# Score buffers of an attention kernel in one PSUM tile, with a table for the order of all engines

## The chip, the core and the metric

The kernel runs on one core of a Trainium2 chip. A core has engines that each work through their own queue of instructions in order: TensorE (PE; its weight loads, PEld, run beside its matmuls), VectorE (DVE), ScalarE (ACT), GpSimd (POOL) and SyncE (SP), whose queue only starts transfers here. An instruction that has to wait for another engine holds up everything behind it in its own queue. The metric is the device time of one execution in microseconds (us); lower is better.

## What is computed

Plain attention for 8 batches of 8 heads, 512 positions and 64 dimensions, float32 in and out:

```python
scale = 1.0 / np.sqrt(q.shape[-1])
scores = np.einsum('bhqd,bhkd->bhqk', q, k) * scale
scores = scores - scores.max(axis=-1, keepdims=True)
attn = np.exp(scores)
attn = attn / attn.sum(axis=-1, keepdims=True)
return np.einsum('bhqk,bhkd->bhqd', attn, v).astype(np.float32)
```

## The kernel before

The 64 heads are taken two at a time: 32 pairs, numbered 0 to 31, with heads a and b. For each pair SP loads q, k and v (256 KB each). POOL casts them to 16 bits. PE transposes q and k (line 558), DVE copies the transposes out of PSUM (L571), and PE computes scores.

A block of scores is 128 keys by 512 queries of one head. Two blocks are a *group*, two PSUM banks of 512 columns each, and all further work goes by groups. They are numbered 0 to 128; the last two are the two halves of one group of scores. Two matmuls write a group (L598). Then it is read in one of two ways:

- ScalarE takes the exponential of all 1024 columns in one instruction and writes 16-bit weights `pt` (L602). The first groups have their own lines (L801).
- For 16 of the groups VectorE does it instead. The list `ON_DVE` names them. One instruction, called *raise* here (`raise_`, L625), reads the scores from PSUM and writes `pd`, and five *passes* (L642 to L665), from and to SBUF, turn `pd` into two factors `pe` and `pd` of the exponential.

PE multiplies the weights with v (L704; v carries a column of ones, so the sums of the weights come along). DVE takes the reciprocal of the sums (L671) and multiplies (L676), and SP stores the result. For the very last head the products land in a tile `o_last` (L720, L734).

PSUM has eight banks. Three buffers of two banks hold scores; two single banks are shared by transposes and products. So at most three groups of scores exist at once, and the matmuls of a group wait until the group three before it has been read. Each of the three buffers is a tile of its own from a pool:

```python
ps_st = ctx.enter_context(tc.tile_pool(name="ps_st", bufs=3, space=bass.MemoryType.PSUM))
...
st = ps_st.tile([P, 2, S], FP32, tag="st", name=f"st_{m}")
```

Waits are not written in the kernel. A layer below it looks at which instruction writes and reads which tile, and puts in a wait on a semaphore wherever two engines touch the same tile in a way that it takes for a dependence. An instruction that comes later in the program waits for the earlier one, never the other way round.

The order of each queue is the order in which the program issues its instructions. The class `Plan` makes it: it steps through an imagined time with a cost for each kind of step and writes down a list of steps, such as "scores of group 40" or "raise of group 39". A step "scores" issues the two matmuls and at once the ScalarE exponential. A step "raise" issues the VectorE read.

Of the kernel before, what the change touches and what calls it, by code (L numbers as in the profile page):

```python
# [17 lines left out]
class Plan:  # L18

    SLOT, EXP, EXP_DONE, EXP_FIXED = 216, 853, 181, 64  # L20
    INTO, OUT_OF = 96, 96
    TRANSPOSE, V_UNIT = 222, 128
    TO_ACT, TO_DVE, TO_PE = 220, 210, 60

    COPY, NORM, RAISE = (601, 690), (50, 133), (1132, 1215)
    RECIPROCAL = 115
    SCALE, PRODUCT, EXTRA = 333, 600, 29
    COPY_1 = (400, 190)
    NORM_COLUMN, PASS_DONE = 67, 115
    PASSES = (SCALE, SCALE, PRODUCT, SCALE, PRODUCT)  # L30
    BITS = 2
    NEEDS = (None, None, 0, 2, 3)
    FIRST_EXP = 5000
    STEP = 5
    CALM, KEEN = 9000, 4
    FIRST_UNIT = 4
    KNOWN, OVER = (13, 15, 18, 20, 22, 24, 27, 42, 50, 61, 69, 97), 6
    ON_DVE = (5, 10, 16, 25, 28, 39, 44, 54, 63, 66, 74, 81, 91, 96, 103, 116)

    LATE_NORM, LATE_COPY, HURRY, SOON, BACKLOG = 700, 1500, 800, 160, 600  # L40
    LATE_MUL, WAIT = 400, 200
    SLACK, AHEAD = 0, 2

    CAST, CAST_PORT, CAST_DONE, TO_POOL = 557, 475, 130, 150
    SCALE_PORT, PRODUCT_PORT, GAP, REACH = 271, 537, 20, 5
    FIRST_LAND, LOAD, STORE, LATENCY, ISSUE = 5200, 752, 376, 2300, 470
    QUEUED, URGENT = 3500, 16
    PAIRED, STORE_ISSUE = 18, 520
    RAW, QK16, NV, NU = 7, 5, 12, 112
    PAIR, DUEK, DUEV, DUEL, PRE = 3300, 3550, 6000, 5000, 0  # L50

    def __init__(self, groups, pairs, first):
        self.groups, self.pairs = groups, pairs
        self.pe, self.act, self.dve = 7000, self.FIRST_EXP, 6300
        self.pool, self.port, self.dma = 4600, 4600, self.FIRST_LAND
        self.m, self.tiled = first, True
        self.read = []
        self.exps = {}
        for m in range(first):
            self.act += self.EXP + self.EXP_FIXED  # L60
            self.exps[m] = self.act + self.EXP_DONE
            self.read.append(self.exps[m])
        self.tq = {0: 5800}
        self.transposed = {0: 5800}
        self.next_t = 1
        self.part_t = 0
        self.banks = [5100, 5800]
        self.todo = [(g, h) for g in range(pairs) for h in range(2)]
        self.last = self.todo.pop()
        self.last_part = 0  # L70
        self.head = None
        self.units = self.FIRST_UNIT
        self.member = {b: m for m, grp in enumerate(groups) for b in grp}
        self.ready = []
        self.passes = []
        self.passed = {}
        self.raised = set()
        self.steps = []
        self.busy_dve = 0
        self.order, self.paired = [], 0  # L80

        late = {grp[0][0] for m, grp in enumerate(groups) if m in self.ON_DVE}
        due = []
        for g in range(pairs):
            scores = 5000 + self.PAIR * g
            if g:
                due += [(scores - self.DUEK, g, "k"), (scores - self.DUEK + 10, g, "q")]
            due.append((scores + self.DUEV + (self.DUEL if g in late else 0), g, "v"))
        self.due = sorted(due)
        self.uncast = list(self.due)  # L90
        self.casts = []
        self.landed, self.cast_done = {}, {}
        self.first_loads = [(g, n) for _, g, n in self.due if g < self.RAW]
        self.first_loads += [(self.RAW, "k"), (self.RAW, "q")]
        for x in self.first_loads:
            self.dma += self.LOAD
            self.landed[x] = self.dma
        self.loads, self.stores, self.stored = [], [], []
        self.sp = 1650 + 470 * len(self.first_loads)

    def note(self, t, *what):
        self.steps.append((t, len(self.steps)) + what)

    def trigger(self, t):

        ops = self.ops
        if not ops or ops[-1][1] <= t - 300:  # L110
            return 1, None
        n = len(ops) - 1
        while (
            n > 0
            and len(ops) - n < self.REACH
            and not ops[n][2]
            and ops[n][0] - ops[n - 1][1] <= self.GAP
        ):
            n -= 1
        if n > 0 and ops[n][0] - ops[n - 1][1] <= self.GAP:  # L120
            n -= 1
        return len(ops) - n, ops[n][1]

    def emit(self, t, back, after):
        _, g, n = self.uncast.pop(0)
        shared = (g, n) == (1, "q")
        self.note(t, "cast", g, n, back if t > self.CALM else 0)
        if not shared:
            self.casts.append((g, n, t if after is None else after + self.TO_POOL))
        if g + self.RAW < self.pairs:  # L130
            self.loads.append((g + self.RAW, n))

    def fits(self, t, soon=0):
        if not self.uncast:
            return False
        _, g, n = self.uncast[0]
        if n != "v" and g >= self.QK16 and self.transposed.get(g - self.QK16, 1e9) > t:
            return False
        return self.landed.get((g, n), 1e9) <= t + soon

    def step_pool(self, t):
        if self.uncast and self.uncast[0][1:] != (1, "q") and not self.casts and self.pool <= t:
            quiet = not self.passes and self.port <= t and not any(x[1] == "raise" for x in self.ready)
            if self.fits(t) and (quiet or self.uncast[0][0] - self.PRE < t):
                self.emit(t, 1, None)
        if self.casts and self.pool <= t and self.port <= t:
            g, n, after = self.casts[0]
            if after <= t and self.landed.get((g, n), 1e9) <= t:
                self.casts.pop(0)
                begin = max(self.pool, self.port, after, self.landed[(g, n)])  # L150
                self.pool = begin + self.CAST
                self.port = begin + self.CAST_PORT
                self.cast_done[(g, n)] = begin + self.CAST + self.CAST_DONE

    def step_sp(self, t):
        if self.sp > t or (self.loads and self.dma > t + self.QUEUED):
            return
        urgent = len(self.stores) > self.URGENT
        if self.loads and not urgent:
            g, n = self.loads[0]  # L160
            if self.cast_done.get((g - self.RAW, n), 1e9) <= t:
                self.loads.pop(0)
                self.note(t, "load", g, n)
                self.dma = max(self.dma, t + self.LATENCY - self.LOAD) + self.LOAD
                self.landed[(g, n)] = self.dma
                self.sp = t + self.ISSUE
                return
        if self.stores and self.stores[0] <= t:
            both = self.both()
            if both and (len(self.stores) < 2 or self.stores[1] > t):  # L170
                return
            heads = 2 if both else 1
            self.note(t, "store", heads)
            self.dma = max(self.dma, t + self.LATENCY - heads * self.STORE) + heads * self.STORE
            for _ in range(heads):
                self.stores.pop(0)
                self.stored.append(self.dma)
            self.paired += heads - 1
            self.sp = t + self.STORE_ISSUE

    def both(self):

        n = len(self.stored)
        g, h, u = self.order[n]
        return (
            self.paired < self.PAIRED
            and g < self.pairs - 2
            and h == 0
            and n + 1 < len(self.order)
            and self.order[n + 1][0] == g  # L190
            and u % self.NU + 8 <= self.NU
        )

    def room(self, t, u):
        heads = (u - self.NU - self.FIRST_UNIT + 3) // 4
        return heads <= 0 or len(self.stored) >= heads and self.stored[heads - 1] <= t

    def free(self, n=0):
        m = self.m + n
        if m >= len(self.groups):  # L200
            return 1e9
        g = self.groups[m][0][0]
        return max(0 if m < 3 else self.read[m - 3], self.tq.get(g, 1e9))

    def for_dve(self, m):
        return m in self.ON_DVE
# [692 lines left out]
```

## Time and profile before

| | |
|---|---|
| time, median of 3 runs (lowest, highest) | 113.97 us (113.85, 114.29) |
| the profiled execution: its time | 113.92 us |
| its span, first to last instruction | 112.1 us |
| mean granted TensorE clock | 0.994 |
| PE busy | 103.2 us (92% of the span) |
| DVE busy | 100.8 us (90%) |
| ACT busy | 105.5 us (94%) |
| POOL busy | 65.9 us (59%) |
| moved by DMA | 33.84 MB, mean 302 GB/s |

Profiled time and span differ by 1.8 us, which lie around the first and last instruction. A group row of the profile gives line, engine, operation, tile written and read, shapes and count; behind the first bar the busy time in us and the mean duration of one in ns; behind the second the time that the engine stood idle just before, and what ended that. Durations of instructions that follow each other closely overlap, so a busy time can be less than count times mean.

### The profile page before, as it was taken

The numbers are of one execution on the slowest core, as the hardware profiler recorded it, in microseconds if no ns is written. First come the engines' busy times: TensorE is split into PE (matmuls) and PEld (weight loads), VectorE is DVE, ScalarE is ACT, GpSimd is POOL, SyncE is SP. The second block draws the span as 40 slices with busy tenths as digits, with TensorE's granted clock in tenths as the row PEclk, the third lists the DMA queues.
The fourth block names the chain that finished last, engine by engine and source line by source line (L and its number), as shares of the span: only waits on it lengthen the run. The fifth ranks groups of instructions, "written<-read, shape, count | busy, mean of one in ns | idle before, by whom it ended". The sixth has DMA issues, their size and how long they took to land.

```text
span 112.1 us, 4408 instructions
## 1 busy us (share of the span) xinstructions
PE 103.2 (92%) x1728; PEld 69.4 (62%) x1728; DVE 100.8 (90%) x227; ACT 105.5 (94%) x118; POOL 65.9 (59%) x127
## 2 busy tenths in 40 slices
PE   7978889999799998999989999899999999999980
PEld 7634555766367766658647767577557577675660
DVE  1647999999999999999999999999999999997390
ACT  4599999999999999999999999999999999999970
POOL 2147768549756886495594786876784855600000
PEclk9999999999999999999999999999999999999997
DMA  3999999999999999999999999999999974142354
GB/s 106 276 359 353 345 350 347 355 336 349 345 347 336 341 346 343 354 364 375 370 358 382 350 355 377 354 372 362 343 366 305 349 245 143 52 141 99 97 167 161
DMA packets 35093, 33.84 MB, mean 302 GB/s; under 512 B 2304, under 2 KB 35072, under 8 KB 35072
## 3 DMA queue, kind: packets, MB, share of 16 engines
q1 hardware_dynamic: 34496, 33.04, 90.4%
q10 hardware_dynamic: 576, 0.52, 1.4%
q8 instruction: 13, 0.21, 0.8%
q14 instruction: 8, 0.07, 0.2%
HBM read 25.17 MB, written 8.39 MB: 299 GB/s over the span
## 4 chain that ended last, share of the span: by engine, by line
DVE 39%; PE 24%; DMA 15%; issue 8%; POOL 7%; SPq 3%; ACT 2%; POOLq 0%; ACTq 0%
PE o L704 13%; DMA v<-in_v_dram 10%; PE st L598 8%; DVE pd L625 8%; DVE tqk L571 7%; DVE ring L676 7%; DMA q<-in_q_dram 5%; DVE m L659 4%; POOL qkp L525 4%; DVE pd L665 4%; POOL vp L515 3%; PE tp L558 2%; SPq L509 2%; DVE m L642 2%; DVE pe L651 2%
## 5 line engine op out<-in xcount | busy, mean ns | idle before, releaser
L602 ACT ACTIVATE pt<-st 128x1024 f16<-128x1024 f32 (+1 forms) x110 | 100.3, 1144 | 0.2 <-PE st L598 0.2
L704 PEld LDWEIGHTS <-pt 128*128 128x128 f16 x880 | 38.8, 98 | 12.1 <-issue 10.2
L704 PE MATMUL o<-vp,pt 128*128 128x65 f16 x880 | 45.3, 194 | 0.4 <-POOL vp L515 0.2
L598 PE MATMUL st<-tqk 64*128 64x512 f16 (+1 forms) x250 | 41.7, 380 | 2.6 <-ACT pt L602 1.4
L525 POOL CAST qkp<-k 128x512 f16<-128x512 f32 x31 | 22.2, 717 | 11.3 <-DVE rc L671 5.3
L525 POOL CAST qkp<-q 128x512 f16<-128x512 f32 x30 | 21.7, 725 | 9.0 <-DVE rc L671 5.3
L515 POOL CAST vp<-v 128x512 f16<-128x512 f32 x32 | 21.4, 679 | 9.2 <-PE st L598 2.4
L676 DVE TENSOR_TENSOR ring<-o,rc 128x448 f32<-128x448 f32 (+2 forms) x37 | 22.3, 606 | 0.4
L704 PE MATMUL o<-vp,pe 128*128 128x65 f16 x128 | 21.8, 194 | 0.0
L704 PE MATMUL o<-vp,pd 128*128 128x65 f16 x128 | 21.7, 192 | 0.0
L558 PE MATMUL tp<-ident,qkp 128*128 128x128 f16 x248 | 19.6, 220 | 1.6 <-DVE tqk L571 0.8
L558 PEld LDWEIGHTS <-qkp 128*128 128x128 f16 x248 | 14.4, 97 | 9.9 <-issue 4.6
L571 DVE COPY tqk<-tp 128x1024 f16<-128x1024 f16 x30 | 20.3, 683 | 0.0
L625 DVE TENSOR_SCALAR pd<-st 128x1024 uint16<-128x1024 f32 x16 | 19.5, 1216 | 0.7 <-PE st L598 0.7
L598 PEld LDWEIGHTS <-tqk 64*128 64x128 f16 x250 | 10.7, 93 | 11.8 <-issue 4.6
L704 PEld LDWEIGHTS <-pe 128*128 128x128 f16 x128 | 12.5, 98 | 3.4 <-issue 3.3
L704 PEld LDWEIGHTS <-pd 128*128 128x128 f16 x128 | 12.5, 98 | 0.0
L659 DVE TENSOR_TENSOR m<-m 128x1024 f16<-128x1024 f16 x16 | 11.0, 685 | 0.0
L665 DVE TENSOR_TENSOR pd<-pd,m 128x1024 f16<-128x1024 f16 x16 | 10.9, 684 | 0.0
L671 DVE RECIPROCAL rc<-o 128x7 f32<-128x7 f32 (+2 forms) x37 | 7.4, 199 | 2.6 <-PE o L704 2.4
L661 DVE TENSOR_SCALAR m<-m 128x1024 f16<-128x1024 f16 x16 | 6.7, 418 | 0.1
L651 DVE TENSOR_SCALAR pe<-pd 128x1024 uint16<-128x1024 uint16 x16 | 6.6, 411 | 0.0
(51 smaller groups left out, 34.9 us busy)
## 6 DMA issues: line engine op xcount, KB each, us to landing
v<-in_v_dram SPq DMA_DIRECT2D x32, 256.0 KB, 5.8
k<-in_k_dram SPq DMA_DIRECT2D x31, 256.0 KB, 5.8
q<-in_q_dram SPq DMA_DIRECT2D x31, 256.0 KB, 5.9
out_dram<-ring SPq DMA_DIRECT2D x18, 256.0 KB, 5.5
out_dram<-ring SPq DMA_DIRECT2D x25, 128.0 KB, 2.2
k<-in_k_dram ACTq DMA_DIRECT2D x2, 128.0 KB, 2.8
q<-in_q_dram SPq DMA_DIRECT2D x2, 128.0 KB, 2.6
out_dram<-ring ACTq DMA_DIRECT2D x2, 128.0 KB, 1.9
```

What stands on the lines that cost most here:

```text
L515: return nc.gpsimd.tensor_copy(out=vps[g % NV][:, :, :, 0:D], in_=raw[g]["v"][:, :, :, :])
L525: return nc.gpsimd.tensor_copy(out=dst, in_=src[:, :, :, :])
L558: reads[g] = nc.tensor.transpose(tps[g][:, n, i, :], qkp[g][:, n, i, :], ident)
L571: nc.vector.tensor_copy(out=tqk[g][:, :, :], in_=tps.pop(g).rearrange("p n i c -> p n (i c)"))
L598: nc.tensor.matmul(st[:, x, cols], kc, qc[:, cols], start=True, stop=True)
L602: ins = nc.scalar.activation(out=pt[:, :, cols], in_=st[:, :, cols], func=EXP, scale=scale, bias=SHIFT)
L625: nc.vector.tensor_scalar(out=r["pd"][:, :, :], in0=r["st"][:, :, :], scalar1=BITS, scalar2=BIAS, op0=AluOp.mult, op1=AluOp.add,)
L651: ins = nc.vector.tensor_scalar(out=r["pe"][:, :, :], in0=u[:, :, :], scalar1=0x7C00, scalar2=None, op0=AluOp.bitwise_and,)
L659: ins = nc.vector.tensor_tensor(out=m16, in0=m16, in1=m16, op=AluOp.mult)
L665: ins = nc.vector.tensor_tensor(out=u16, in0=u16, in1=m16, op=AluOp.mult)
L676: nc.vector.tensor_tensor(out=ring[:, u % NU : u % NU + n, :], in0=o[:, x : x + n, 0:D], in1=rcs.pop(u)[:, 0:n].broadcast_to([P, n, D]), o ...
L704: nc.tensor.matmul(os[u // 7][:, u % 7, :], part[:, y * P : (y + 1) * P], vps[g % NV][:, h, c, :], start=(n == 0), stop=(n == len(parts) - 1),
```

## The change

1. The three score buffers become one PSUM tile `sts` of six banks; group m uses its third number (m + 1) mod 3 (`banks`).
2. With one tile, the layer that puts in waits would tie every access to every other. A new helper `at` notes which third an instruction touches and declares pairs on different thirds independent, where one of the two is a TensorE instruction and the other is not.
3. At three places (`JOINED`: groups 69, 99, 102) a group and the next one get one exponential of 2048 columns, which runs when both have been scored. Their weights lie in two double buffers; the single ones go from 24 to 20.
4. `Plan` is gone. A table of letters gives the steps: `S` scores, `T` transposes, `V` products, `R` raise, `C` copy, `K` cast, `N` and `M` reciprocal and multiply, `G` and `W` load and store, small letters passes. `ON_DVE` is still 16 groups, partly others (82 where it was 81, for instance).
5. In the last pair the two heads' blocks come in another order, and the last products go to a third of `sts`.

```diff
-    ON_DVE = (5, 10, 16, 25, 28, 39, 44, 54, 63, 66, 74, 81, 91, 96, 103, 116)
+    ON_DVE = (5, 11, 16, 25, 29, 39, 45, 54, 60, 66, 74, 82, 89, 97, 109, 117)
+    JOINED = (69, 99, 102)
+    SINGLES, DOUBLES = 20, 2
+    LAST_PAIR = "a0b0 a1b1 a2a3 b2b3"
+    STEPS = (
+        "SKKTTKCSKSTRKSTSCVKVaSVcSKSNMTbTdSKCKRSTKTSCSKVVfTeVTSKCSGVVRVKSGKVVNGkSKMSVGhTVgTGSiSCG"
...
+    sts = ps_st.tile([P, 3, 2, S], FP32, tag="st", name="sts")
+    touched = []
+
+    def banks(m):
+        return sts[:, (m + 1) % 3], (m + 1) % 3
+
+    def at(ins, *where, tied=False):
+        pe = nc.tensor.engine
+        for other, there, also in touched[-64:]:
+            apart = there.isdisjoint(where) and not also
+            if apart and (other.engine == pe) != (ins.ins.engine == pe):
+                tc.declare_no_dep(ins.ins, other, reason="other banks")
+        touched.append((ins.ins, set(where), tied))
...
-        st = ps_st.tile([P, 2, S], FP32, tag="st", name=f"st_{m}")
+        st, bank = banks(m)
...
-            nc.tensor.matmul(st[:, x, cols], kc, qc[:, cols], start=True, stop=True)
+            at(nc.tensor.matmul(st[:, x, cols], kc, qc[:, cols], start=True, stop=True), bank)
...
+        if own == 0 or first_of:
             return
+        if second_of:
+            low, step = min(bank, (bank + 2) % 3), 1 if bank else 2
+            ins = nc.scalar.activation(
+                out=last["two"][:, :, :, :],
+                in_=sts[:, low : low + step + 1 : step],
+                func=EXP,
+                scale=scale,
+                bias=SHIFT,
+            )
+            at(ins, bank, (bank + 2) % 3)
...
     def raise_(m):
...
+        ins = nc.vector.tensor_scalar(
+            out=r["pd"][:, own:2, :],
+            in0=r["st"][:, own:2, :],
...
+        at(ins, r["bank"])
+        dve(ins)
```

What stands in the queues, at two places. First VectorE, about two thirds through the program, around the raise of group 81 in the kernel before. In a row stand the line, the operation, the tile written and the tiles read (with the group in the name), the size, and the semaphores waited for: `PE`, `DVE`, `Activation` for ScalarE.

```order
L661 TENSOR_SCALAR m_66_1752<-m_66_1752 128x1024 [waits DVE_49]
L642 TENSOR_SCALAR m_74_1903<-pd_74_1756 128x1024
L665 TENSOR_TENSOR pd_66_1575<-pd_66_1575,m_66_1752 128x1024 [waits DVE_49]
L625 TENSOR_SCALAR pd_81_1911<-st_81_1909 128x1024 [waits PE_49]
L671 RECIPROCAL rc_133_1966<-o_19_1875 128x7
L651 TENSOR_SCALAR pe_74_1755<-pd_74_1756 128x1024
L671 RECIPROCAL rc_140_1974<-o_20_1922 128x7 [waits PE_49]
```

The same place of VectorE's queue in the changed kernel, around the raise of group 82:

```order
L402 TENSOR_SCALAR m_66_1666<-m_66_1666 128x1024 [waits DVE_49]
L412 RECIPROCAL rc_133_1837<-o_19_1792 128x7 [waits PE_49]
L406 TENSOR_TENSOR pd_66_1510<-pd_66_1510,m_66_1666 128x1024 [waits DVE_49]
L362 TENSOR_SCALAR pd_82_1851<-sts_100 128x1024 [waits Activation_49]
L417 TENSOR_TENSOR ring_85<-o_19_1792,rc_133_1837 128x448 [waits DVE_49]
L412 RECIPROCAL rc_140_1896<-o_20_1832 128x7 [waits PE_49]
```

The raise (L625, now L362) waited for TensorE alone; now it waits for ScalarE. The semaphore value in the built program is the one that the exponential of group 83 brings. Every one of the 16 raises waits for a ScalarE exponential now (seven of them for PE besides), and none did before.

Second ScalarE, the exponentials around the same place. Before:

```order
L602 ACTIVATE pt_80_1865<-st_80_1864 128x1024 [waits PE_49,Activation_49]
L602 ACTIVATE pt_82_1918<-st_82_1917 128x1024 [waits PE_49,Activation_49]
L602 ACTIVATE pt_83_1945<-st_83_1944 128x1024 [waits PE_49,Activation_49]
L602 ACTIVATE pt_84_1970<-st_84_1969 128x1024 [waits PE_49,Activation_49]
L602 ACTIVATE pt_85_1977<-st_85_1976 128x1024 [waits PE_49,Activation_49]
```

And in the changed kernel:

```order
L331 ACTIVATE pt_80_1774<-sts_100 128x1024 [waits PE_49,Activation_49]
L331 ACTIVATE pt_81_1827<-sts_100 128x1024 [waits PE_49,Activation_49]
L331 ACTIVATE pt_83_1843<-sts_100 128x1024 [waits PE_49,Activation_49]
L331 ACTIVATE pt_84_1871<-sts_100 128x1024 [waits DVE_49,PE_49]
L331 ACTIVATE pt_85_1887<-sts_100 128x1024 [waits PE_49,Activation_49]
```

The exponential of group 84 has got a wait for VectorE, and its value is the one that the raise of group 82 brings. Sixteen exponentials have such a wait, one behind each raise. (A wait of an exponential for `Activation` is for the one that wrote the same weight buffer some 20 groups earlier.)

More of the change, by code (lines that the diff above doesn't have):

```diff
@@ L579, in scores @@
         cols = slice(256 * half, 256 * half + 256) if half >= 0 else slice(0, S)
-        st = ps_st.tile([P, 2, S], FP32, tag="st", name=f"st_{m}")
+        st, bank = banks(m)
+        own = 0 if on_dve and m not in Order.SPLIT else 1 if on_dve else 2
+        first_of, second_of = m in Order.JOINED, m - 1 in Order.JOINED
         if on_dve:
-            tiles = {n: dpool.tile([P, 2, S], U16, tag=n, name=f"{n}_{m}") for n in ("pe", "pd")}
-            raised[m] = {"st": st, **tiles}
-            parts = [tiles[n].bitcast(FP16) for n in ("pe", "pd")]
+            raised[m] = {"st": st, "own": own, "bank": bank}
+        if own == 0:
+            pass
         elif half == 1:
             pt = last["pt"]
-        else:
-            pt = last["pt"] = ppool.tile([P, 2, S], FP16, tag="pt", name=f"pt_{m}")
+        elif first_of:
+            last["two"] = ppool.tile(
+                [P, 2, 2, S], FP16, tag="pt2", name=f"pt_{m}", bufs=Order.DOUBLES
+            )
+            pt = last["two"][:, int(bank == 2)]
+        elif second_of:
+            pt = last["two"][:, int(bank != 0)]
+        else:
+            pt = last["pt"] = ppool.tile(
+                [P, 2, S], FP16, tag="pt", name=f"pt_{m}", bufs=Order.SINGLES
+            )
         for x, (g, c, h) in enumerate(grp):
@@ L713, in last_values @@
         if part == 0:
-            last["o"] = ps_st.tile([P, 2, S], FP32, tag="st", name="o_last")[
-                :, 0, 0 : NI * (D + 1)
-            ].rearrange("p (x d) -> p x d", x=NI)
+            st, _ = banks(len(groups))
+            last["o"] = st[:, 0, 0 : NI * (D + 1)].rearrange("p (x d) -> p x d", x=NI)
         half, late = ((0, 0), (1, 0), (0, 1), (1, 1))[part]
@@ L727, in last_values @@
                 )
+                for halves in () if late else last["exps"]:
+                    tc.declare_no_dep(ins.ins, halves, reason="other banks")
     def finish():
@@ L749, in busy @@
     def busy(dst, n):
-        nc.tensor.matmul(dst[:, 0:n], ones[:, 0:P], ones[:, 0:n], start=True, stop=True)
+        return nc.tensor.matmul(dst[:, 0:n], ones[:, 0:P], ones[:, 0:n], start=True, stop=True)
     def first_pair():
@@ L770, in first_pair @@
         nc.scalar.copy(k16[:, 1], tk[:, 1])
-        st0, pka, st1 = (
-            ps_st.tile([P, 2, S], FP32, tag="st", name=f"st_{n}") for n in ("0a", "ka", "1")
-        )
+        st0, pka, st1 = (sts[:, n] for n in range(3))
         pqa = ps_x.tile([P, 8, P], FP16, tag="x0", name="tp_qa")
@@ L820, in first_pair @@
         nc.vector.tensor_copy(out=qt[:, 1, 0:2], in_=pqb[:, 0:2])
-        pts = [ppool.tile([P, 2, S], FP16, tag="pt", name=f"pt_{m}") for m in range(3)]
+        pts = [ppool.tile([P, 2, S], FP16, tag="pt", name=f"pt_{m}", bufs=Order.SINGLES) for m in range(3)]
         for m in range(3):
@@ L824, in first_pair @@
                 blocks[b] = [pts[m][:, x, :]]
[L825 to L828 removed]
+        first_scores(0, 0, 0, 0, 256, pts[0], 0, 256)
+        first_scores(1, 0, 0, 256, 512, pts[0], 0, 256)
+        first_scores(2, 0, 1, 0, S, pts[1], 0, S)
         pkb = ps_x.tile([P, 8, P], FP16, tag="x0", name="tp_kb")
@@ L835, in first_pair @@
         nc.vector.tensor_copy(out=qt[:, 1, 2:4], in_=pqb[:, 2:4])
-        st2 = ps_st.tile([P, 2, S], FP32, tag="st", name="st_2")
         for n in range(4):
-            busy(st2[:, 0], P)
-        first_scores(st2, 1, 0, 0, S, pts[2], 0, S)
+            at(busy(sts[:, 0, 0], P), 0)
+        first_scores(0, 1, 0, 0, S, pts[2], 0, S)
         first.update(kt=kt, qt=qt)
     with tc.manual_schedule():
-        plan = Plan(groups, NP, 3)
-        steps = plan.run()
+        order = Order()
         first_loads()
-        for g, name in plan.first_loads:
+        for g, name, _ in order.read(order.FIRST):
             load(g, name)
@@ L866 @@
         }
-        for what, *args in steps:
+        for what, *args in order.steps():
             do[what](*args)
```

565 lines of the change are left out of this document (138 added, 427 removed), and 13 rows, old and new, of tables (CASTS, HEADS, LOADS).

## Prediction

> **What bounds the kernel now.** I read the busy times of the page first, then its slices, then ScalarE's groups with tile shapes kept apart, then the order of time on ScalarE and VectorE, and last the waits.
>
> ```profile
> PE 103.2 (92%) x1728; PEld 69.4 (62%) x1728; DVE 100.8 (90%) x227; ACT 105.5 (94%) x118; POOL 65.9 (59%) x127
> ACT  4599999999999999999999999999999999999970
> ```
>
> Three engines are over 90% busy, but only ScalarE is full in every slice from the fourth to the third from the end. Its groups say how:
>
> ```profile
> L602 ACT ACTIVATE pt<-st 128x1024 f16<-128x1024 f32 x108 | 99.4, 1153 | 0.2 <-PE st L598 0.2
> L801 ACT ACTIVATE pt<-st 128x1024 f16<-128x1024 f32 x2 | 1.9, 1038 | 0.0
> L602 ACT ACTIVATE pt<-st 128x512 f16<-128x512 f32 x2 | 1.1, 616 | 0.0
> ```
>
> One exponential takes 1153 ns from start to end, but 108 of them take 99.4 us together: 99.4 / 108 = 0.920 us from start to start, because each begins before the one ahead has ended. The column of idle time shows 0.2 us for the whole kernel. So ScalarE bounds it: whatever keeps ScalarE waiting between about 5 us and 108 us is added to the time, one to one, and a shorter queue there is taken off.
>
> VectorE's 16 raises matter next:
>
> ```profile
> L625 DVE TENSOR_SCALAR pd<-st x16: 1208/1216/1225, 9.4 to 97.7; 128x1024 uint16<-128x1024 f32 x16
> 9.21 11.16 ACT L602 ACTIVATE pt<-st 128x1024 f16<-128x1024 f32 x12 [0.18 <-PE st L598]
> 13.69 1.21 DVE L625 TENSOR_SCALAR pd<-st 128x1024 uint16<-128x1024 f32 x1
> ```
>
> A raise takes 1.216 us (the middle figure of the three). The two rows of the timeline show one raise, 13.69 to 14.90 us, in the middle of an unbroken run of twelve exponentials, 9.21 to 20.37 us. Both engines read PSUM at once here, in different buffers, and ScalarE doesn't stop. All 16 raises lie hidden in this way.
>
> **The change part by part.**
>
> *The waits between ScalarE and VectorE.* This is the term that decides. The helper `at` declares two accesses independent only where one is TensorE's and the other is not. A ScalarE exponential and a VectorE raise are both "not TensorE", so for that pair nothing is declared, and both now read the one tile `sts`. The rows of the order show what the layer below makes of it: each raise waits for the last exponential issued ahead of it, and the next exponential issued waits for the raise. Neither needs the other's data. With separate tiles neither wait was there.
>
> So at each of the 16 places the two engines meet. ScalarE finishes exponential A; only then may the raise run; only when it is done may exponential B start. What is queued behind them: behind B all further exponentials; behind the raise, while it waits, VectorE's copies, reciprocals and products. The price of a meeting needs the time in which one engine answers another, for which these rows stand:
>
> ```profile
> 4.06 0.41 ACT L769 CAST q<-q 128x256 f16<-128x256 f32 x1 [0.56 <-DMA q<-in_q_dram]
> 4.51 0.13 PEld L789 LDWEIGHTS <-q 128*128 128x128 f16 x2 [0.42 <-ACT q L769]
> 6.65 0.62 POOL L525 CAST qkp<-k 128x512 f16<-128x512 f32 x1 [2.98 <-DMA k<-in_k_dram]
> 7.32 0.23 PEld L558 LDWEIGHTS <-qkp 128*128 128x128 f16 x4 [0.89 <-POOL qkp L525]
> ```
>
> ScalarE's cast ends at 4.47 and TensorE starts at 4.51; POOL's ends at 7.27 and TensorE starts at 7.32. I take 0.05 us for an answer. From the start of A to the start of B it was 0.920 us. Now it is A in full, an answer, the raise in full, an answer: 1.153 + 0.05 + 1.216 + 0.05 = 2.469 us. The loss is 1.549 us for each meeting, and 16 x 1.549 = 24.8 us.
>
> Bounds for this price, since no meeting is in the trace of before. From below: the raise alone stands in the way, nothing else, 16 x 1.216 = 19.5 us. It cannot be less, because B may not start before the raise has ended, the raise not before A has, and A's successor had started before A's end until now. From above: VectorE is not at the raise when A ends, and is late by one of its usual operations. Its commonest costly ones are
>
> ```profile
> L571 DVE COPY tqk<-tp 128x1024 f16<-128x1024 f16 x30 | 20.3, 683 | 0.0
> L676 DVE TENSOR_TENSOR ring<-o,rc 128x448 f32<-128x448 f32 (+2 forms) x37 | 22.3, 606 | 0.4
> L659 DVE TENSOR_TENSOR m<-m 128x1024 f16<-128x1024 f16 x16 | 11.0, 685 | 0.0
> L665 DVE TENSOR_TENSOR pd<-pd,m 128x1024 f16<-128x1024 f16 x16 | 10.9, 684 | 0.0
> L671 DVE RECIPROCAL rc<-o 128x7 f32<-128x7 f32 (+2 forms) x37 | 7.4, 199 | 2.6 <-PE o L704 2.4
> L661 DVE TENSOR_SCALAR m<-m 128x1024 f16<-128x1024 f16 x16 | 6.7, 418 | 0.1
> L651 DVE TENSOR_SCALAR pe<-pd 128x1024 uint16<-128x1024 uint16 x16 | 6.6, 411 | 0.0
> L642 DVE TENSOR_SCALAR m<-pd 128x1024 uint16<-128x1024 uint16 x16 | 6.5, 408 | 0.0
> ```
>
> With 0.606 us more at each meeting the sum is 24.8 + 9.7 = 34.5 us.
>
> Is VectorE late? Between two raises I added up what the new table puts on each engine, with the means of these rows. ScalarE has 95 exponentials between the first raise and the last (92 single, 3 joined), about 90 us; VectorE's work there, without the raises, is 83.2 us. Of the 15 stretches only one has more for VectorE: nine exponentials, 8 x 0.920 + 1.153 = 8.51 us, against 8.58 us. So VectorE is normally there first and waits, and I add 0.07 us for that stretch.
>
> *What stands behind a raise on the other queues.* The score matmuls into the raised third wait for the raise, as they did before. In the table the exponential right behind a raise never needs anything that VectorE does after the raise; its scores are issued ahead. The second one mostly needs the raised third itself: its matmuls run while the first exponential does, so they cost nothing as long as they fit into 0.920 us:
>
> ```profile
> L598 PE MATMUL st<-tqk 64*128 64x512 f16 (+1 forms) x250 | 41.7, 380 | 2.6 <-ACT pt L602 1.4 <-DVE pd L625 0.7 <-DVE tqk L565 0.5
> ```
>
> They take 0.380 us, since the two run side by side. At one place, behind the raise of group 29, they wait for a VectorE copy too: 0.683 + 0.05 + 0.380 + 0.05 = 1.163 us against 0.920 + 0.05, so 0.2 us is added.
>
> *Three joined exponentials.* They save the fixed part of three instructions. The half-size ones show it:
>
> ```profile
> 5.20 0.60 ACT L801 ACTIVATE pt<-st_0a 128x512 f16<-128x512 f32 x1 [0.43 <-PE st_0a L794]
> 5.69 0.59 ACT L801 ACTIVATE pt<-st_0b 128x512 f16<-128x512 f32 x1
> 6.17 1.95 ACT L801 ACTIVATE pt<-st 128x1024 f16<-128x1024 f32 x2
> ```
>
> The starts 5.20, 5.69 and 6.17 are 0.485 us apart for 512 columns, and twice that is 0.97 us, where 1024 columns take 0.920. A join saves 0.05 us, three save 0.15 us. On the other side a joined exponential holds two thirds of `sts` for some 1.8 us; one group is ready in the last third, and the next two must be scored within its 0.920 us. Two groups are 0.76 us of matmuls. That fits if PE comes to them at once; I take no cost and bound it at 1 us for all three. The Trainium skill (ScalarE: Activation LUTs, section "What ACT_TABLE_LOAD costs") gives an exponential with immediate scale and bias a fixed 186 ns, of which about 93 ns overlap between neighbours; by that a join saves 0.09 us and three 0.28 us. The rows give 0.05 and I stay with them; the sum would change by 0.13 us.
>
> *Waits by third, the table, the last pair.* The matmuls wait for the same readers as with three separate buffers, so nothing is won there; ScalarE stood idle for them for 0.2 us in all, and no rearrangement can give back more. The work is the same: 16 raises, as many casts, copies, products and loads. PE has 103.2 us of work, and with some 137 us to do it in, none of it binds; the same holds for VectorE and the loads. The end is
>
> ```profile
> 97.19 11.30 ACT L602 ACTIVATE pt<-st 128x1024 f16<-128x1024 f32 x13
> 107.98 0.74 PEld L720 LDWEIGHTS <-pt 128*128 128x128 f16 x16
> 109.55 0.33 SPq L740 DMA_DIRECT2D out_dram<-obl  x1
> ```
>
> After the last exponential (108.49) come the last products, a division and the store. The new last pair reorders what comes ahead of the last exponential, and the same kind of products is left behind it: I take 0, bounded by plus or minus 0.4 us.
>
> The sum against the profiled execution: 113.92 + 24.8 + 0.07 + 0.2 - 0.15 = 138.8 us. That execution lies 0.05 us under the median of the runs, which is nothing beside the terms.
>
> **The rivals.** A measurement of this kernel can tell 0.5%, 0.6 us, from no change.
>
> *Late meetings, slower still.* VectorE comes late by an operation at most raises, because a reciprocal or copy in its queue waits for TensorE, which waits for an exponential that is itself held back. For it: VectorE is 90% busy and works in order. Against it: the sums by stretch, and that the waits for TensorE came to 2.4 us, two waits, in the row of L671. The time is 113.92 + 34.5 - 0.15 = 148.3 us.
>
> *The meetings cost about half.* Where ScalarE would have waited for TensorE anyway, part of a meeting falls into that wait. The idle column of L602, 0.2 us, speaks against it: there is next to nothing to fall into. At 0.78 us each it would be 126.3 us.
>
> *The reads go side by side, a shade faster.* If the waits were met before either engine arrives, exponentials and raises would overlap as in the timeline above, and the joins and the 0.2 us of idle time would be won: 113.92 - 0.15 - 0.2 = 113.6 us; with everything in the tail's bound, 113.2 us. This decides if the value that a raise waits for is reached before the raise's turn, so if the exponential issued ahead of it has run long ago. But ScalarE works with its scores just ready (three thirds, one in use), and a group is raised within two exponentials of being scored, so it has not. The Trainium skill (PSUM — Partial Sum Buffer, section "Specifications (TRN2)") says that ScalarE and VectorE can read PSUM in parallel at full bandwidth as long as they use different banks. By that rule the chip itself needs no meeting here, and the timeline rows above agree. What stops the engines is the wait written into the program, not the memory.
>
> **How the numbers follow.** The forecast of 138.8 us has 0.82; late meetings 0.10; half the price 0.05; side by side 0.03. The range takes in the lower bound of the price, 113.92 + 19.5 - 0.15 = 133.3 us, so 133, and reaches up to near the late case, 147. Faster and the same both need the last rival: 0.01 and 0.02; slower has 0.97.
>
> **What would show it.** In the profile of the changed kernel ScalarE's busy time should stay near 109 us (105.5 and 16 ends of 0.23 us that no longer overlap), a share of about 80%, and some 16 x 1.3 = 21 us of its idle time should end with the raise on VectorE. VectorE should wait for ScalarE's exponential ahead of raises. The timeline should show no exponential beside any raise. Wrong would be idle time of ScalarE that TensorE ends, or raises beside exponentials with a time under 133 us; idle time well over 1.4 us at each raise would mean late meetings.

## The result, and the profile after

| | before | after |
|---|---|---|
| median of six runs each, us | 114.06 (113.8 to 114.29) | 140.47 (138.98 to 140.78) |
| ratio, 95% interval | | 1.2283 (1.2212 to 1.2353) |
| profiled execution, us | 113.92 | 140.5 |
| its span, us | 112.1 | 138.7 |
| mean granted TensorE clock in it | 0.994 | 0.945 |

The forecast was 138.8 us in a range of 133 to 147, slower with a chance of 0.97. The ratios here and below leave out every execution that took more than 1.5% longer than the fastest one of its kernel, while medians and ranges include them.

The page of the changed kernel: the line of busy times, two of the lines in 40 slices (ScalarE's busy share and, as PEclk, the granted TensorE clock, both in tenths), and its two groups for the exponentials and the raises (busy us, mean ns of one, then the idle time ahead of them and what ended it).

```profile
PE 112.3 (81%) x1728; PEld 73.8 (53%) x1728; DVE 104.1 (75%) x227; ACT 107.7 (78%) x115; POOL 67.4 (49%) x127
ACT  4786696979678696969696687969696997896980
PEclk9999559999959999999999699999999999999997
L331 ACT ACTIVATE pt<-sts 128x1024 f16<-128x1024 f32 (+1 forms) x104 | 97.4, 1033 | 24.6 <-DVE pd L362 20.3
L362 DVE TENSOR_SCALAR pd<-sts 128x1024 uint16<-128x1024 f32 x16 | 19.6, 1225 | 21.3 <-ACT pt L331 21.3
```

ScalarE was full in nearly every slice; now most slices lie between 6 and 9. ScalarE and VectorE have hardly more work than before (107.7 against 105.5 us busy, 104.1 against 100.8). TensorE counts 9 us more, 112.3 against 103.2; part of it ran at half clock, which the last section takes up. No engine is over 81% busy. The time has gone into waiting, and the groups say which: ScalarE's idle time of 0.2 us has become 24.6 us, of which the raise ends 20.3.

The waits (us in total, times, the longest):

```profile
DVE pd L362 <- ACT pt L331: 21.3, 16, 2.0
ACT pt L331 <- DVE pd L362: 20.3, 15, 1.4
ACT pt L331 <- PE sts L315: 4.1, 4, 1.4
```

VectorE waits at all 16 raises for the exponential, ScalarE at 15 of them for the raise. The sixteenth wait of ScalarE, 1.35 us like the others and ending at 17.54 us, is put down to TensorE, and so stands in the third row. One meeting in order of time, first ScalarE's rows, then VectorE's (start, duration, and in brackets the idle time ahead and what ended it):

```profile
103.75 1.07 ACT L331 ACTIVATE pt<-sts 128x1024 f16<-128x1024 f32 x1
106.18 1.02 ACT L331 ACTIVATE pt<-sts 128x1024 f16<-128x1024 f32 x1 [1.35 <-DVE pd L362]
107.10 1.87 ACT L322 ACTIVATE pt<-sts 128x2048 f16<-128x2048 f32 x1
...
104.86 1.23 DVE L362 TENSOR_SCALAR pd<-sts 128x1024 uint16<-128x1024 f32 x1 [1.30 <-ACT pt L331]
```

The exponential ends at 104.82, the raise starts at 104.86 and ends at 106.09, the next exponential starts at 106.18. From start to start that is 2.43 us where it was 0.92 before; VectorE has stood idle for 1.30 us ahead of its raise.

### The profile page after: what moved, and what is told of

The parts are those of the page before. It is cut to its first block, busy times and chain, and to the rows that moved or that the text cites. A ratio compares the mean times of both kernels' runs of the same rounds, so it can differ in the third digit from the quotient of the medians.

```text
span 138.7 us, 4370 instructions
## 1 busy us (share of the span) xinstructions
PE 112.3 (81%) x1728; PEld 73.8 (53%) x1728; DVE 104.1 (75%) x227; ACT 107.7 (78%) x115; POOL 67.4 (49%) x127
## 4 chain that ended last, share of the span: by engine, by line
ACT 40%; PE 23%; DVE 19%; issue 9%; DMA 4%; POOL 1%; SPq 1%; ACTq 0%; DVEq 0%
ACT pt L331 39%; DVE pd L362 14%; PE o L445 11%; PE sts L315 8%; PE tp L248 4%; DMA q<-in_q_dram 4%; DVE ring L417 2%; DVE tqk L261 1%; ACT pt L322 1%; POOL vp L205 1%; SPq L489 1%; DVE m L383 1%; DVE pd L406 0%; POOL qkp L215 0%; DVE tqk L255 0%
## 5 line engine op out<-in xcount | busy, mean ns | idle before, releaser
L331 ACT ACTIVATE pt<-sts 128x1024 f16<-128x1024 f32 (+1 forms) x104 | 97.4, 1033 | 24.6 <-DVE pd L362 20.3
L315 PE MATMUL sts<-tqk 64*128 64x512 f16 (+1 forms) x250 | 45.8, 397 | 19.6 <-DVE pd L362 12.3
L445 PE MATMUL o<-vp,pt 128*128 128x65 f16 x880 | 51.0, 198 | 0.9 <-DVE tqk L261 0.4
L445 PEld LDWEIGHTS <-pt 128*128 128x128 f16 x880 | 41.9, 100 | 18.5 <-issue 14.6
L215 POOL CAST qkp<-k 128x512 f16<-128x512 f32 x31 | 23.9, 772 | 27.4 <-DVE rc L412 6.3
L362 DVE TENSOR_SCALAR pd<-sts 128x1024 uint16<-128x1024 f32 x16 | 19.6, 1225 | 21.3 <-ACT pt L331 21.3
L248 PE MATMUL tp<-ident,qkp 128*128 128x128 f16 x248 | 23.1, 232 | 1.5 <-DVE ring L417 0.6
L215 POOL CAST qkp<-q 128x512 f16<-128x512 f32 x30 | 19.8, 664 | 9.0 <-DVE pd L362 3.1
L445 PE MATMUL o<-vp,pe 128*128 128x65 f16 x128 | 23.1, 199 | 0.0
L248 PEld LDWEIGHTS <-qkp 128*128 128x128 f16 x248 | 15.7, 103 | 10.0 <-issue 4.7
```

What stands on the lines that cost most here:

```text
L215: return nc.gpsimd.tensor_copy(out=dst, in_=src[:, :, :, :])
L248: reads[g] = nc.tensor.transpose(tps[g][:, n, i, :], qkp[g][:, n, i, :], ident)
L315: at(nc.tensor.matmul(st[:, x, cols], kc, qc[:, cols], start=True, stop=True), bank)
L331: ins = nc.scalar.activation(out=pt[:, 0:own, cols], in_=st[:, 0:own, cols], func=EXP, scale=scale, bias=SHIFT)
L362: ins = nc.vector.tensor_scalar(out=r["pd"][:, own:2, :], in0=r["st"][:, own:2, :], scalar1=BITS, scalar2=BIAS, op0=AluOp.mult, op1=AluOp.add,
L445: nc.tensor.matmul(os[u // 7][:, u % 7, :], part[:, y * P : (y + 1) * P], vps[g % NV][:, h, c, :], start=(n == 0), stop=(n == len(parts) - 1),
```

## Experiments

All times are medians, with the range. A ratio is to the kernel before on the same chip: 113.82 us for experiments 1, 2, 3 and 7, 113.96 us for 4 to 6, 113.83 us for 8 to 10.

**1. The missing pair declared.** The condition of `at` is widened to any two engines; nothing else is changed.

```diff
-            if apart and (other.engine == pe) != (ins.ins.engine == pe):
+            if apart and other.engine != ins.ins.engine:
```

> The changed kernel with one condition altered in the helper: ScalarE and VectorE accesses to different thirds of the score tile are declared independent too. A raise then waits only for the exponential of the group three before it, which used the same third, and an exponential only for the raise of the group three before. If the 16 meetings are the whole cause, the 26.6 us go and the time is 113.6 us (113.0 to 114.6), ScalarE's idle time at raises falls from 21.6 us to under 1 us, and raises lie beside exponentials again. If the table, the single tile or the joined exponentials cost by themselves (the two further stalls of 1.3 and 1.2 us in ScalarE's queue are theirs), 2 to 3 us of it stay: 116 to 117 us. If the loss has little to do with these waits, it stays over 130 us.

Measured 114.54 us (114.36 to 115.4) against 113.82: ratio 1.0071 (1.0047 to 1.0096). One condition carries 25.9 of the 26.4 us. The timeline of this kernel, ScalarE first, then one raise:

```profile
8.17 51.60 ACT L331 ACTIVATE pt<-sts 128x1024 f16<-128x1024 f32 x56
59.55 1.99 ACT L322 ACTIVATE pt<-sts 128x2048 f16<-128x2048 f32 x1
...
17.15 1.21 DVE L362 TENSOR_SCALAR pd<-sts 128x1024 uint16<-128x1024 f32 x1
```

There are 56 exponentials in one unbroken stretch of 51.60 us, 0.92 us each, and the raise at 17.15 runs in the middle of it: both engines read the one tile, in different thirds, and neither stops. So the loss is made of waits in the program. The Trainium skill (PSUM — Partial Sum Buffer, section "Specifications (TRN2)") says that ScalarE and VectorE read PSUM in parallel when they use different banks; this timeline agrees, 1.21 us for the raise beside exponentials at their usual pitch.

**2. The table on three tiles.** The same table and queues, with three lasting tiles in place of one, no declarations, and no joined exponentials (a joined one can't cross two tiles).

```diff
-    sts = ps_st.tile([P, 3, 2, S], FP32, tag="st", name="sts")
+    sts = [ps_st.tile([P, 2, S], FP32, tag=f"st{n}", name=f"st_{n}") for n in range(3)]
```

> The table of orders alone: three separate score tiles, no joined exponential, 24 single weight buffers, nothing declared independent. If the meetings are the cause, the table is about as good as the planner's order: 113.9 us (113.2 to 114.8). If the new order is what costs, it stays well above 116 us.

Measured 114.37 us (114.09 to 114.82): ratio 1.0051 (1.0029 to 1.0072). Table and new order together cost about 0.55 us (0.3 to 0.8 by the interval). Its ScalarE, in one row of the timeline:

```profile
8.11 100.94 ACT L323 ACTIVATE pt<-st 128x1024 f16<-128x1024 f32 x110
```

**3. The meetings alone, in the kernel before.** Each raise is made to wait for the last exponential issued ahead of it and the next exponential for the raise; planner, tiles and order stay.

```diff
+        if "raise" in last:
+            tc.add_manual_dep(ins.ins, last.pop("raise").ins.name, SYNC, reason="meet")
+        last["exp"] = ins
...
+        tc.add_manual_dep(ins.ins, last["exp"].ins.name, SYNC, reason="meet")
+        last["raise"] = ins
```

> The kernel before, with its own order, tiles and exponentials, and one thing added: each of the 16 raises waits for the last exponential issued ahead of it, and the next exponential issued waits for the raise. If the meetings are the cause, 16 of them at 1.45 us (the spacing of exponentials around a raise in the changed kernel, 2.37 us, less 0.92) are 23.2 us: 137.1 us, and up to 141 us if some matmuls come late as in the changed kernel. If tile, joins or table are needed for the loss, it stays under 125 us.

Measured 142.5 us (141.59 to 144.19): ratio 1.2487 (1.242 to 1.2554). The waits in this kernel:

```profile
DVE pd L628 <- ACT pt L602: 24.4, 16, 2.7
ACT pt L602 <- DVE pd L628: 20.3, 15, 1.4
ACT pt L602 <- PE st L598: 3.6, 6, 0.9
```

The waits of ScalarE are almost number for number those of the changed kernel: 20.3 us in 15, a sixteenth of 1.4 us that is put down to a reciprocal (L676), and a few for late scores. So the meetings are also enough by themselves. The median is above the expected 137.1 to 141 us. The profiled execution took 141.59 us. With the price worked out below, 113.8 + 16 x 1.47 + 3.6 us of late scores are 140.9 us; the other 0.7 us are not broken down.

**4 and 5. One wait of the two.** First only the raise waits for the exponential, and the exponential behind it is free; then the other way round.

```diff
+            act, dv = nc.scalar.engine, nc.vector.engine
+            free = (other.engine, ins.ins.engine) == (dv, act)
+            if apart and (free or (other.engine == pe) != (ins.ins.engine == pe)):
```

> The changed kernel with one half of each meeting kept: the raise waits for the last exponential issued ahead of it, but the exponential behind the raise doesn't wait for the raise. If ScalarE's wait is the price, most of the 26.6 us go. VectorE still stands idle ahead of each raise, and it has little slack: 100.8 us busy in the kernel before, within some 103 us. Sixteen waits of up to 1.3 us, as in the changed kernel (21.3 us in all), would make VectorE's queue 122 us long, so 118 to 126 us if VectorE becomes the bound, 114 to 116 us if its waits shrink as ScalarE runs on without stopping. If both halves cost alike, about 127 us.

> The other half: the raise may start as soon as its scores are there, and the next exponential issued waits for the raise to end. A raise then starts while ScalarE still has up to two exponentials to do, 1.84 us, against 1.23 us for the raise; if it starts at once, ScalarE hardly waits: 114 to 117 us. If VectorE comes to the raise late by an operation (0.6 us) each time, 16 x 0.6 is 9.6 us: 122 to 125 us. If the two halves cost alike, about 127 us.

With the raise's wait alone: 133.66 us (131.94 to 135.27), ratio 1.1677 (1.1601 to 1.1754), above everything that had been expected. With the exponential's wait alone (`(act, dv)` in the second line): 116.88 us (116.54 to 117.22), ratio 1.0255 (1.0224 to 1.0287), as expected. The waits of the first:

```profile
DVE pd L364 <- ACT pt L333: 16.3, 15, 1.7
ACT pt L333 <- PE sts L317: 13.3, 22, 1.6
PE sts L317 <- DVE pd L364: 11.4, 13, 1.2
```

and of the second:

```profile
ACT pt L333 <- DVE pd L364: 1.7, 5, 0.5
```

In the first no exponential waits for a raise, and ScalarE is held up all the same: the raise runs late by up to 1.7 us, the scores of the group that gets its third are late behind it (11.4 us), and the exponentials wait for these scores (13.3 us). In the second the raise runs when its scores are there, long before the exponential behind it, which then waits for it in 5 places out of 16, 1.7 us in all. The halves cost 19.7 and 2.9 us, together less than the 26 us of both: the raise's wait is the dear one, and the exponential's wait is dear only because the raise is late.

**6. Every second meeting.** Eight of the 16 raises are declared independent of the exponentials of other thirds. (The lines of `at` that keep a list of these raises are left out here.)

```diff
-        at(ins, r["bank"])
+        at(ins, r["bank"], free=Order.ON_DVE.index(m) % 2 == 1)
```

> The changed kernel with every second raise, eight of sixteen, declared independent of exponentials on other thirds; the other eight meet as before. If each meeting has its own price, eight cost 8 x 1.45 = 11.6 us and perhaps one of the two further stalls: 125 to 127 us. If a few bad places or a queue that runs ever later made the loss, it is far from half: under 120 or over 132 us.

Measured 128.9 us (128.75 to 128.96): ratio 1.1308 (1.1283 to 1.1333), above the expected 125 to 127. The group of single exponentials with shapes kept apart:

```profile
L336 ACT ACTIVATE pt<-sts 128x1024 f16<-128x1024 f32 x102 | 95.8, 1058 | 13.5 <-DVE pd L367 10.8 <-PE sts L320 2.2 <-ACT pt L336 0.2
```

Eight waits of 10.8 us together are 1.35 us each, the same as in the changed kernel: a meeting's price was the same with eight as with sixteen. The expectation left out the 0.5 us of the table and had room for one late stall; here late scores make 2.2 us. 113.96 + 0.55 + 8 x 1.47 + 2.2 = 128.5 us.

**7 and 8. No joined exponentials,** once without meetings (experiment 1's condition) and once with them.

```diff
-    JOINED = (69, 99, 102)
-    SINGLES, DOUBLES = 20, 2
+    JOINED = ()
+    SINGLES, DOUBLES = 24, 2
```

> As the run with both kinds of pairs declared independent, and without the joined exponentials (24 single weight buffers). If a join saves 0.05 to 0.09 us and costs nothing, this is 0.15 to 0.27 us slower than that run: 113.8 to 114.0 us. If a joined exponential makes the following scores late, as the stall of 1.24 us behind the first one in the changed kernel suggests, this is faster than that run, by up to 1 us.

> The changed kernel with its 16 meetings and without joined exponentials (24 single weight buffers). If the stall of 1.24 us behind the first joined exponential comes from the join holding two thirds, it is gone whatever the granted clock, and the time is 139 us where the clock stays near 0.98. If it comes from the drop of the granted clock there, the time stays at 139 to 141 us with the clock, and the stall appears at another place where the clock has dropped.

Without meetings: 114.51 us (113.97 to 115.33) against 114.54 with the joins. With meetings: 140.31 us (139.82 to 142.28) against 140.47. The joins move nothing that can be measured, either way. In the changed kernel a late score (1.24 us) stands at 79.03, soon behind the join of group 69, which made the join a suspect. The same place without it, in the timeline of experiment 8:

```profile
78.26 3.79 ACT L331 ACTIVATE pt<-sts 128x1024 f16<-128x1024 f32 x4 [1.09 <-PE sts L315]
```

The stall is still there, 1.09 us, so it isn't the join's. (The one of 1.30 us at 42.05 is gone, though no join lies ahead of it in either kernel; the last section comes back to that.)

**9. One exponential earlier.** The raise waits for the last but one exponential issued ahead of it in place of the last; the next exponential still waits for the raise.

```diff
+            last_act = next((o for o, _, _ in reversed(touched) if o.engine == nc.scalar.engine), None)
+            free = ins.ins.engine == nc.vector.engine and other is last_act
+            if apart and (free or (other.engine == pe) != (ins.ins.engine == pe)):
```

> The changed kernel, but a raise waits for the last but one exponential issued ahead of it instead of the last; the exponential behind it still waits for the raise. The raise may then run beside one exponential. If the price of a meeting is the time from the end of the exponential waited for to the start of the next one that may run, each falls from 1.45 us by one exponential's 0.92 us to 0.53 us, and 16 cost 8.5 us on top of the 114.5 us without meetings: 123 us (121.5 to 124.5). If VectorE is late anyway, the raise doesn't start earlier and it stays over 130 us; if one exponential of room is enough to hide the raise, it is 115 to 117 us.

Measured 123.46 us (123.13 to 125.07): ratio 1.0826 (1.0759 to 1.0892), where 123 was expected. Its waits:

```profile
ACT pt L333 <- DVE pd L364: 7.3, 16, 0.6
DVE pd L364 <- ACT pt L333: 6.7, 11, 1.1
```

ScalarE still waits at all 16 places, but for 0.46 us and not 1.35. Each has lost 0.89 us, about one pitch, as the working of the price says: a meeting costs what is left of exponential, raise and answers once one pitch more lies beside the raise.

**10. The table on fresh tiles.** As experiment 2, with a pool that hands out a tile for each group, as the kernel before has it, and the first pair's lines as there.

```diff
-        return sts[:, (m + 1) % 3], (m + 1) % 3
+        return ps_st.tile([P, 2, S], FP32, tag="st", name=f"st_{m}"), 0
```

> The table of orders with the tiles of the kernel before: each group of scores has a tile of its own from a pool of three buffers, no joined exponential, the first pair as before. No raise waits for an exponential and no exponential for a raise, not even for those of the group three before. If those old waits, though met long ago, slow ScalarE's queue by the 0.5 us that the run of the table with three lasting tiles was slower, this is as fast as the kernel before: 113.6 to 114.1 us. If the order itself costs the 0.5 us, it stays at 114.4 us.

Measured 114.34 us (113.73 to 115.03): ratio 1.0034 (1.0 to 1.0067). How tiles are handed out makes no difference to experiment 2. Of the 26.4 us, some 0.5 us go with the new order by experiments 2 and 10, though the interval of this one reaches down to nothing. In experiment 2's row 110 exponentials take 100.94 us; in the profile of before the same 110 take 100.51 us (7.98 to 108.49). Why they take a little longer without idle time between them was not found. No kernel tried here beats the one before.

## Why the prediction was right, point by point

**The mechanism.** It was as forecast: waits between ScalarE and VectorE at 16 places, which neither needs. Declaring the pair independent takes away 26 of 26.4 us (experiment 1), adding the waits to the kernel before brings at least as much (experiment 3), and each meeting costs the same (experiment 6). The signs named for it are there too: ScalarE 107.7 us busy, a share of 78%; 20.3 us of its idle time ended by the raise, and 1.35 us more; and none of the 16 raises beside an exponential. That ScalarE's waits are added to the time one to one is borne out by the sum below. It could not be taken for granted: the chain on the page of the kernel before runs through VectorE for 39% of the span and through ScalarE for 2%, and the prediction doesn't discuss that.

**The price of a meeting** was 1.549 us and is about 1.47: 1.04 for the exponential in full (the mean of the 102 single ones of 1024 columns), 1.35 idle, less 0.92, so 23.5 us for 16 and not 24.8. The term was sized too high because 1.153 us, the mean of an exponential before, holds time in which it already counts while its neighbour is still at work. The exponentials right ahead of a raise take 1.02 to 1.13 us in the changed kernel, those right behind one 1.02. Against that the answer from VectorE to ScalarE took 0.09 us where 0.05 was set; the one from ScalarE to VectorE took 0.04.

**Who comes late.** The forecast had VectorE normally first, and it was so every time: it waited 16 times out of 16. The stretch for which 0.07 us was added can't be seen, and "late meetings" is out. The sum of VectorE's work between raises, 83.2 us, was too high as well: it adds up whole durations, and in the changed kernel's profile VectorE is busy there for some 73 us, because its operations overlap each other too. But the story that a raise merely stands in ScalarE's way was too simple. Experiments 4 and 5 show that the lateness of the raise does the harm, through ScalarE directly in the changed kernel, and through the scores of the next group if that direct wait is taken away.

**The copy behind the raise of group 29** was priced at 0.2 us. Rows of ScalarE in the timeline of the changed kernel, the first two behind meetings:

```profile
31.55 3.77 ACT L331 ACTIVATE pt<-sts 128x1024 f16<-128x1024 f32 x4 [1.35 <-DVE pd L362]
36.67 4.08 ACT L331 ACTIVATE pt<-sts 128x1024 f16<-128x1024 f32 x4 [1.35 <-DVE pd L362]
42.05 4.69 ACT L331 ACTIVATE pt<-sts 128x1024 f16<-128x1024 f32 x5 [1.30 <-PE sts L315]
79.03 3.79 ACT L331 ACTIVATE pt<-sts 128x1024 f16<-128x1024 f32 x4 [1.24 <-PE sts L315]
```

The run at 36.67 is the one behind that raise: 4.08 us where an undisturbed four takes 3.77, so 0.31 us. Not all of it is the copy's. In the profile of experiment 8 the same four take

```profile
37.46 3.91 ACT L331 ACTIVATE pt<-sts 128x1024 f16<-128x1024 f32 x4 [1.35 <-DVE pd L362]
```

and there TensorE ran at full clock, where the changed kernel has half clock from 38.1 us on. So 0.14 us stand against the 0.2 of the forecast, and the other 0.17 us appear only with the slow clock.

**The joins** were to save 0.05 us each. In the timeline above a join starts at 107.10, and behind it stands

```profile
108.85 1.03 ACT L331 ACTIVATE pt<-sts 128x1024 f16<-128x1024 f32 x1
```

That is 1.75 us from start to start for two groups, against 2 x 0.92: 0.09 us saved. Here the figure of the Trainium skill (ScalarE: Activation LUTs, section "What ACT_TABLE_LOAD costs"), 0.09 us, was the better one. The bound of 1 us for their cost wasn't needed.

**What the sum lacked.** The last two rows of the fence above have stalls of 1.30 and 1.24 us, in which ScalarE waits for scores. The prediction named idle time of ScalarE that TensorE ends as a sign against it, and there is some, 2.5 us beside the meetings; no term stood for it. And the table itself was set at 0 within 0.4 us, where experiments 1 and 2 show 0.72 and 0.55. With the right sizes: 114.36 (experiment 1's profiled execution) + 16 x 1.47 + 0.31 + 1.30 + 1.24 = 140.7 us, against 140.5 in the profile. So the forecast of 138.8 us is near in part by luck: a price that was 1.3 us too high stood in for half of the late scores that weren't foreseen.

**Half price and side by side.** There was nothing for a meeting to fall into: 1.35 us of idle time at each. And the memory does let both engines read side by side, as experiment 1 shows; the program doesn't.

## What to carry to other kernels

Where two buffers are put into one tile, list every pair of engines that touches it, readers too, and see in the built program which pair has got a wait: here two readers of different thirds were tied, and that cost 23%. Price a false wait between two engines in order as one instruction in full, the other in full and two answers, less the pitch they had before, times the places; a wait that starts one instruction earlier is cheaper by a whole pitch. And when a bound engine gets gaps, look at what the gaps do to the engines behind it, not only at the gaps.

## What the hardware did that was not expected

The granted TensorE clock fell to half in stretches of the changed kernel; before, it was 1.00 in every window from 10 to 108 us. Windows of its profile, one in which TensorE stood still and three at half clock (window, length, busy us and instructions of TensorE, its weight loads, VectorE, ScalarE and GpSimd, then granted clock, DMA share and GB/s), and its score matmuls from 38.1 to 41.4 us and, below, from 43 to 47 us:

```profile
35.30:37.20 1.90, 0.00 (x0) 0.00 (x0) 1.85 (x3) 0.55 (x2) 0.56 (x1) 1.00 0.96 259
14.20:21.00 6.80, 6.51 (x52) 3.23 (x50) 4.49 (x7) 5.45 (x7) 3.95 (x6) 0.50 1.09 340
38.10:41.40 3.30, 3.30 (x41) 2.46 (x40) 3.13 (x7) 2.58 (x3) 0.81 (x3) 0.50 0.68 219
75.70:79.00 3.30, 3.30 (x47) 2.77 (x45) 2.61 (x7) 2.09 (x2) 1.52 (x4) 0.50 0.93 325
L315 PE MATMUL sts<-tqk 64*128 64x512 f16 x4 | 1.0, 618 | 0.0
L315 PE MATMUL sts<-tqk 64*128 64x512 f16 x10 | 1.8, 384 | 0.0
```

A score matmul takes 618 ns in the middle stretch and 384 ns soon after it, at full clock. The stalls of 1.30 us (42.05) and 1.24 us (79.03) lie right behind the last two stretches; behind the first there is none. That suggests that the slow clock made the scores late. Experiment 8 bears on it: up to the first join its queues are those of the changed kernel, only with more weight buffers, but in its profile the slow stretches lie elsewhere:

```profile
22.80:26.10 3.30, 3.21 (x27) 1.61 (x27) 3.10 (x7) 3.18 (x4) 1.12 (x3) 0.50 1.09 348
36.10:38.00 1.90, 0.00 (x0) 0.00 (x0) 1.85 (x4) 0.55 (x2) 0.56 (x1) 1.00 0.66 177
38.90:42.20 3.30, 3.30 (x68) 2.34 (x66) 3.30 (x9) 3.30 (x4) 0.81 (x3) 1.00 0.73 242
74.00:77.30 3.30, 3.02 (x34) 2.19 (x34) 2.75 (x6) 2.85 (x3) 1.36 (x3) 0.50 1.05 354
28.14 2.86 ACT L331 ACTIVATE pt<-sts 128x1024 f16<-128x1024 f32 x3 [0.47 <-PE sts L315]
37.46 8.60 ACT L331 ACTIVATE pt<-sts 128x1024 f16<-128x1024 f32 x9 [1.35 <-DVE pd L362]
```

At the place where the changed kernel had half clock from 38.1 us, the clock is full here (68 matmuls in 3.3 us, not 41), nine exponentials run through, and the stall of 1.30 us isn't there. Behind the slow stretch from 22.8 us there is a new stall of 0.47 us, and behind the one from 74 us the stall of 1.09 us. So the stalls come and go with the clock at the same places of the queues. In experiment 6, too, its late scores (0.85, 0.49 and 0.90 us, ending at 26.85, 37.28 and 40.13) lie in or behind its half-clock stretches, 22 to 25.3 and 35.7 to 39 us. These are executions set side by side; no kernel that held the clock up by other means was tried. It agrees that the runs of the changed kernel at a mean clock of 0.975 and 0.988 took 138.98 and 138.99 us, those at 0.945 to 0.963 took 140.43 to 140.78, and that experiment 9, profiled at 1.0, came out at its expected time.

The Trainium skill (TensorE: Matmul & The Clock Gate, section "Why this matters for your kernels") asks for no gaps of TensorE over about 3 us. Here they were shorter. The waits of TensorE's queue and of its score matmuls with the longest single wait in them:

```profile
PEld L315 <- DVE tqk L261: 4.4, 4, 2.1
PE sts L315 <- DVE tqk L261: 3.5, 4, 2.0
```

No wait is over 2.1 us, and still the clock was halved for at least 3.3 us at a time. Nor does the longest gap decide by itself: TensorE stands still at 35.3 to 37.2 us in the changed kernel and at 36.1 to 38.0 us in experiment 8, the same place of the queue, and half clock follows about a microsecond later in the one and not in the other. What in these gaps brings the clock down, their sum, their number or the moment at which they fall, stays open.
